# A two-layer hybrid decoder on one core: projection blocks with products of 512 and 256 columns, one more scanning pair, and a new order of the pieces

## The chip, the cores and the metric

The kernel runs on one core of one Trainium2 chip, in one launch. The metric is the device time of the whole program in microseconds; the time before is the median of three runs. In the profile PE is TensorE (matmuls), PEld its weight loads, DVE is VectorE, ACT is ScalarE, POOL is GpSimd and SP is the engine whose queue issues most DMAs.

## What is computed

Two layers on x (256 tokens, 1024 features) with 256 memory tokens. In each layer the normed x is multiplied by one wide weight matrix, whose columns belong to three groups of heads: six stick-breaking heads ("sb"), six MoBA heads ("mb", which at this length is causal softmax attention with rotary embedding), and four heads that attend to the memory tokens ("mem"). Each group is gated by silu of its own gate columns, all are joined and multiplied by w_out, and the result is added to x. A norm closes the program. All of it is float32. Cut to what matters:

```python
for layer in range(DEPTH):                                   # 2
    h = rms_norm(x, norm_g[layer])
    proj = jnp.einsum('btd,dc->btc', h, w_in[layer])         # 1024 x 3584
    sb_q, sb_k, sb_v, sb_g, mb_q, mb_k, mb_v, mb_g, mem_q, mem_g = jnp.split(proj, split_at, axis=-1)
    o_sb = merge_heads(stick_breaking_attention(q, k, v)) * jax.nn.silu(sb_g)
    # per head: z = q k' / 8; log_beta = log_sigmoid(z); log_one_minus = where(past, log_beta - z, 0)
    #   later = reverse cumsum over keys of log_one_minus, less itself
    #   out = where(past, exp(log_beta + later), 0) @ v
    o_mb = merge_heads(moba_attention(partial_rotary(mb_q), partial_rotary(mb_k), mb_v)) * jax.nn.silu(mb_g)
    m = rms_norm(mem, mem_norm_g[layer])
    mk, mv = jnp.split(jnp.einsum('bmd,dc->bmc', m, w_mem_kv[layer]), 2, axis=-1)
    o_mem = merge_heads(memory_attention(mem_q, mk, mv)) * jax.nn.silu(mem_g)
    x = x + jnp.einsum('btc,cd->btd', jnp.concatenate([o_sb, o_mb, o_mem], -1), w_out[layer])
return rms_norm(x, final_norm_g)
```

## The kernel before

**Products in three parts.** A float32 operand is split into two parts of type float32r: hi is the value rounded, lo the rest. A float32 product is made of three: hi*hi, hi*lo and lo*hi, accumulated in one PSUM bank. The activations lie in T tiles of 512 columns per step k of the contraction (eight steps of 128): columns 0 to 255 hold hi for the 256 tokens, 256 to 511 hold lo. Ts lists for each tile its hi half, its lo half and the whole (X[0], X[1], X[2] in the helpers).

**Weights.** w_in, w_mem_kv and w_out come in pieces (one for sb_q, one for sb_g, and so on) in the order that ORDER gives for each layer, then wo0, wo1 and wo2 for the output projection. A piece is cut into chunks of 128 x 768 values (the first four are halves). SP issues their loads, six raw buffers deep; hi_task casts a chunk to hi on ACT or DVE, lo_task makes lo by a subtraction on DVE and then issues the next load. Seven split chunks (tiles hl) can stand ahead of TensorE. At given chunks other loads are put in between: the transposed x (X_AT), the two halves of x (X0_AT, X1_AT) and the constants (CST_AT).

**Blocks.** A piece whose result is wanted transposed (queries and keys of sb and mem, and all gates) is made by T_piece: for each block of 128 of its columns a bank, and in it eight calls of tr_k, each three products of 256 columns. The layer has 18 such blocks, both layers 36. The others (v, and q and k of mb) are made by N_piece, with products of 384 or 256 columns. sb_qk of layer 0 is done first and differently: all six blocks at once, step k by step k, as the weights arrive. Then a block is evacuated: evac_T for queries and keys, gate_evac for gates, by one move on ACT or DVE, and in layer 0 with a multiply by the row norms rbx.

**Attention.** For each pair of heads pair_scores takes two banks and makes the scores, with products on half of the array's rows; pair_task multiplies the weights by V, on half of its columns. SCG and PVG list which pairs are issued together. In layer 0 the sb pairs get the running sum by products with a constant triangle (pair_sums, tiles neg and ah; sb_head does the elementwise part), and give the weights already transposed (wT). In layer 1 the sum is a scan on DVE (scan_head), and the weights are turned as those of the other heads are: 32x32 transposes on DVE into D, a store to DRAM (Z) and four loads back (pair_turn, trip), which SP issues; HALVES names the pairs for which these are eight. The result, times the gate, is split into mxhi and mxlo, the input of the output projection, which takes its eight steps k in the order KORD.

**What sets the order.** All instructions of each engine are issued in an order that a planner finds when the program is built: Sched runs the tasks (generators) against a clock for each engine and a cost for each instruction, with priorities (PRI, P_...), lateness of TensorE tasks (..._LATE), thresholds on free banks (SPARE1, SPARE2, CROWD) and the time at which each buffer is freed. _avail says when a task could go on: from k.t, the end of its last instruction, its inputs and the buffers it asks for. The main task issues all full products in order; before each block it asks for a bank in a step that issues nothing, and its first product is asked for in the next step.

Of the kernel before, what the change touches and what calls it, by code (L numbers as in the profile page):

```python
# [10 lines left out]
AF = mybir.ActivationFunctionType  # L11
OP = mybir.AluOpType
# [15 lines left out]
RAW = 6  # L28
KORD = ((0, 1, 2, 3, 4, 5, 6, 7), (6, 7, 4, 5, 0, 1, 2, 3))
LAT_SAME, LAT_CROSS = 130.0, 240.0  # L30
PE_LATE = 400.0
NORM_LATE = 1234.4
DG_LATE = 544.9
COLD = 3900.0
PRI = {"sb": (44, 10), "mb": (8, -6), "mem": (22, 22)}
P_EV = 37
P_H0 = -8
P_RX = 37
P_M0 = 12
P_RM = 37  # L40
P_M1 = 0
URG = 2
X_AT = {5: 4, 6: 5, 7: 6, 8: 7}
CST_AT = 14
X0_AT = 11
X1_AT = 16
DMA_GBS = 330.0
# [5 lines left out]
TRIP_LAT = 1500.0  # L53
MEM_AT = 0
ORDER = (["sb_qk", "mb_k", "mb_q", "mem_q", "mk", "mv", "sb_v", "mb_g", "sb_g", "mb_v", "mem_g"],
         ["mv", "mk", "mb_q", "mb_k", "mem_q", "sb_q", "sb_k", "mb_v", "mem_g", "mb_g", "sb_g", "sb_v"])
GATES = {"sb_g": ((0,), (1,), (2,)), "mb_g": ((0,), (1,), (2,)), "mem_g": ((0,), (1,))}
SCG = (((("sb", 0), ("sb", 1)), (("mb", 0),), (("mb", 2), ("sb", 2)), (("mb", 1), ("mem", 1)), (("mem", 0),)),
       ((("mb", 1), ("mb", 2), ("mb", 0)), (("mem", 1), ("mem", 0)), (("sb", 0), ("sb", 2)), (("sb", 1),)))
PVG = (((("sb", 0),), (("sb", 1), ("mb", 0), ("mb", 1)), (("sb", 2), ("mb", 2)), (("mem", 0), ("mem", 1))),  # L60
       ((("sb", 2), ("mb", 0)), (("mb", 1), ("mem", 0), ("mem", 1)), (("sb", 0),), (("mb", 2),), (("sb", 1),)))
HOLD = 10396.4
HALVES = [("F", 1, "mb", 1), ("F", 1, "mem", 0), ("F", 0, "mb", 2), ("F", 0, "mem", 1)]
CROWD = 2
SPARE1 = 2
SPARE2 = 1
DVE_W = 554.2
AHEAD = 2
DVE_HI = 671.6
SLACK_PE = 36.4  # L70
SLACK = 89.6

# [24 lines left out]
class Sched:  # L97
# [86 lines left out]
    def run(self):  # L184
        while self.tasks:
            cands = []
            for k in self.tasks:
                prio = k.prio() if callable(k.prio) else k.prio
                best = None
                for eng, cost in k.req["eng"]:  # L190
                    a = self._avail(k, eng)
                    if a is None:
                        continue
                    s = max(a, self.T[eng])
                    if best is None or s + cost < best[0]:
                        best = (s + cost, s, eng)
                if best:
                    cands.append((best[1], prio, best[2], k))
            assert cands, [(k.gen.__name__, k.req) for k in self.tasks]
            s0, _, eng0, _ = min(cands, key=lambda c: (c[0], c[1]))  # L200
            slack = SLACK_PE if eng0 == "pe" else SLACK
            cands = [c for c in cands if c[2] == eng0 and c[0] <= s0 + slack]
            if eng0 == "pe":
                cands = self._by_form(cands)
            _, _, eng, k = min(cands, key=lambda c: (c[1], c[0]))
            if eng == "pe":
                self.form = k.req.get("form", "full")
                self.held.pop(k, None)
            t = self._avail(k, eng)
            bufs = []  # L210
            for tag in k.req.get("alloc", ()):
                b = self.res[tag].best()
                self.res[tag].items.remove(b)
                bufs.append(b[2])
            k.t0 = t
            self._step(k, (eng, bufs))
# [3 lines left out]
def hybrid_trunk(ctx: ExitStack, tc: tile.TileContext, x, mem, norm_g, w_in, w_mem_kv, w_out,  # L220
# [26 lines left out]
    def mm(out, lhsT, rhs, start, stop, **kw):  # L247
        n = _free(rhs)
        half = lhsT.shape[0] == 64 or out.shape[0] == 64
        if lhsT.dtype == FR:  # L250
            c = max(111.0, n * 0.4167 + (20.0 if n > 384 else 13.0))
# [4 lines left out]
        nc.tensor.matmul(out, lhsT=lhsT, rhs=rhs, start=start, stop=stop, **kw)  # L256
# [76 lines left out]
    spare = [sb(f"F{i}", [128, 768]) for i in range(2)]  # L333
    S.res["wT"] = Res([f[:, o:o + 384] for f in spare for o in (0, 384)])
    S.res["Fs"] = Res([])
    S.res["D"] = Res([sb(f"D{i}", [128, 1024]) for i in range(2)])
# [332 lines left out]
    def pair_scores(l, kind, c):  # L669
# [8 lines left out]
        if kind == "mem":  # L678
            regs = [(slice(0, 256), slice(0, 128), slice(0, 256)), (slice(256, 512), slice(128, 256), slice(0, 256))]
        elif kind == "sb" and l == 0:  # L680
# [3 lines left out]
        st, mv_ = (ks[kind], qs[kind]) if kind == "sb" and l == 0 else (qs[kind], ks[kind])  # L684
        for j, (o, a, b) in enumerate(regs):
            for h in range(2):
# [5 lines left out]
                mm(out, st[r, c, a], rhs, j == 0, j == 1)  # L692
        if kind != "sb" or l:
            place[l, kind, c] = len(place)
# [4 lines left out]
    def sb_head(l, h):  # L699
# [14 lines left out]
        stt(a, z, 0.0, a, OP.max, OP.add)  # L714
        e, (hl,) = yield R(("act", 320.0), ("dve", 200.0), alloc=["ah"], cond=lambda: 3 * l + h // 2 <= turn["sb"])
        copy(hl[0], a, e)
# [118 lines left out]
    def pair_task(l, kind, c):  # L835
# [7 lines left out]
        for q, i in group:  # L843
            need += [("wT", l, q, 2 * i), ("wT", l, q, 2 * i + 1)] if q == "sb" and l == 0 else [("F", l, q, i)]
            need.append((VN[q], l))
# [3 lines left out]
        n = 4 if kind == "mem" else 3  # L849
        sums = kind == "sb" and l == 0  # L850
        if sums:
            w2 = [wTs.pop((l, kind, 2 * c + b)) for b in range(2)]
# [3 lines left out]
        for j in range(2):  # L856
            q0 = 0 if j == 0 or kind == "mem" else 128
            for b in range(2):
                out = o[b * 64:b * 64 + 64, q0:256]
                if sums:  # L860
                    rhs = w2[b][:, 256 * j:256 * j + 256 - q0]
# [205 lines left out]
    def main():  # L1067
# [26 lines left out]
        for l in range(DEPTH):  # L1094
# [40 lines left out]
            for kind, n in (("sb", 3), ("mb", 3), ("mem", 2)):  # L1135
                for c in range(n):
                    S.spawn(pair_scores(l, kind, c), PRI[kind][0] + 2)
                    S.spawn(pair_sums(l, c) if kind == "sb" and l == 0 else pair_turn(l, kind, c), PRI[kind][0] + 1)
                    S.spawn(pair_task(l, kind, c), PRI[kind][0])
            if l == 0:  # L1140
# [4 lines left out]
                for k in range(KT):  # L1145
                    if k < 4:
                        groups = [range(3), range(3, 6)] if k < 2 else [range(6)]
                        for g in groups:
                            j, o = p.loc(k, g[0] * 128)
                            o -= g[0] * 128  # L1150
                            steps = [(his, 0, [("hi", j), ("h", 0, "hi", k)]), (his, 1, [("h", 0, k)]),
                                     (los, 0, [("lo", j)])]
                            for w, h, need in steps:
                                prog["cur"] = max(prog["cur"], j)
                                yield R("pe", need=need)
                                for c in g:
                                    mm(accs[c][:, 0:256], w[j % LEAD][:, o + c * 128:o + c * 128 + 128], hT[h][:, k, :],
                                       k == 0 and h == 0 and w is his, False)
# [123 lines left out]
```

## Time and profile before

| | us |
|---|---|
| median of three runs | 274.12 |
| lowest, highest | 274.1, 275.38 |
| profiled execution: device time | 274.33 |
| its span, first to last instruction | 272.6 |
| PE busy | 263.5 |
| DVE busy | 224.0 |
| ACT busy | 194.9 |

The span is what the profile's times are measured in; the device time of the same execution is 1.7 us longer. A group's row reads: line, engine, operation, what it writes from what it reads, shapes, count, then busy time in all, mean ns of one instruction, and the idle time before them with what ended it. A mean of PE holds its pipeline, so the rate of a stream of products is read from the starts in the timeline. A row of the windows has, for each engine, busy us and in brackets the number of instructions, then the granted clock, the busy share of the DMA engines and GB/s.

### The profile page before, as it was taken

How to read it: one execution, taken by the hardware profiler on the slowest of the kernel's cores; microseconds unless marked ns; L12 is line 12 of the kernel's file. 1: busy time of each engine (PE TensorE's matmuls, PEld its weight loads, DVE VectorE, ACT ScalarE, POOL GpSimd, SP SyncE). 2: the span in 40 equal slices, each digit the busy share in tenths (PEclk: the TensorE clock that was granted, in tenths of full speed). 3: DMA queues.
4: the chain of work that ended last, by engine and by line, in shares of the span. 5: the costliest groups of instructions: out<-in, count | busy, mean ns of one | idle time of the engine just before them, and what ended most of it. 6: DMA issues, size and time to landing. Idle time of an engine off the chain costs nothing.

```text
span 272.6 us, 5581 instructions
## 1 busy us (share of the span) xinstructions
PE 263.5 (97%) x1943; PEld 252.8 (93%) x1943; DVE 224.0 (82%) x507; ACT 194.9 (72%) x461; POOL 7.2 (3%) x19
## 2 busy tenths in 40 slices
PE   8999999999979999999999999999999999999991
PEld 5999999999879998998999999999999989988991
DVE  4688986899878999994879587699999999984282
ACT  3578976798897998780875446497989999843053
POOL 0002020200000000000000000000000000000000
PEclk9999999999999999999999999999999999999997
DMA  6999989979954968987294966986798789990004
GB/s 206 353 367 374 390 277 351 301 226 296 265 208 116 268 170 204 340 239 249 74 300 146 303 198 226 273 266 188 248 267 247 257 248 262 315 304 16 2 0 154
DMA packets 49995, 64.74 MB, mean 238 GB/s; under 512 B 4208, under 2 KB 46064, under 8 KB 49968
## 3 DMA queue, kind: packets, MB, share of 16 engines
q1 hardware_dynamic: 48880, 62.29, 73.3%
q0 software_dynamic: 512, 1.31, 1.6%
q10 hardware_dynamic: 576, 0.79, 0.8%
q8 instruction: 15, 0.25, 0.3%
q14 instruction: 12, 0.10, 0.1%
HBM read 56.12 MB, written 8.26 MB: 236 GB/s over the span
## 4 chain that ended last, share of the span: by engine, by line
PE 90%; DMA 4%; DVE 3%; ACT 1%; SPq 0%; issue 0%; DVEq 0%
PE bank L256 90%; DMA raw<-in_w_in_dram 4%; DVE w L781 1%; PE bank L262 1%; DVE st L794 0%; SPq L363 0%; DVE D L828 0%; DVE hl L279 0%; ACT hl L273 0%; ACT ss L275 0%; ACT junk L275 0%; DVE xs L287 0%; DVEq L1278 0%; DVE bank L283 0%; DVE st L803 0%
## 5 line engine op out<-in xcount | busy, mean ns | idle before, releaser
L279 DVE TENSOR_TENSOR hl<-raw,hl 128x768 fp32r<-128x768 f32 (+3 forms) x113 | 101.4, 905 | 12.8 <-ACT hl L273 12.1
L256 PE MATMUL bank<-T,hl 128*128 128x256 f32 x864 | 107.4, 285 | 2.4 <-DVE st L781 2.2
L256 PEld LDWEIGHTS bank<-T,hl 128*128 128x128 f32 x864 | 105.5, 193 | 4.0 <-DVE st L781 2.3
L273 ACT CAST hl<-raw 128x768 fp32r<-128x768 f32 (+3 forms) x101 | 80.1, 802 | 15.1 <-PE bank L256 9.7
L256 PE MATMUL bank<-hl,T 128*128 128x384 f32 (+1 forms) x480 | 81.0, 325 | 0.0
L256 PEld LDWEIGHTS bank<-hl,T 128*128 128x128 f32 x480 | 78.0, 189 | 0.5 <-issue 0.3
L256 PE MATMUL bank<-hl,mxhi 128*128 128x384 f32 (+1 forms) x192 | 45.4, 319 | 0.0
L256 PEld LDWEIGHTS bank<-hl,mxhi 128*128 128x128 f32 x192 | 33.3, 189 | 0.9 <-issue 0.7
L256 PE MATMUL bank<-hl,mxlo 128*128 128x384 f32 (+1 forms) x96 | 30.4, 317 | 0.0
L275 ACT ACTIVATE w<-w,st 128x256 f32<-128x256 f32 (+1 forms) x54 | 22.3, 459 | 1.7 <-DVE st L781 1.1
L275 ACT ACTIVATE junk<-xs 128x384 bf16<-128x384 f32 (+2 forms) x15 | 7.9, 529 | 21.4 <-DVE xs L279 21.0
L275 ACT ACTIVATE ga<-ga 128x256 f32<-128x256 f32 x48 | 19.3, 425 | 0.3 <-DVE ga L283 0.2
L256 PEld LDWEIGHTS bank<-hl,mxlo 128*128 128x128 f32 x96 | 18.1, 189 | 0.0
L828 DVE STREAM_TRANSPOSE D<-w 128x384 f32<-128x384 f32 (+1 forms) x26 | 15.6, 607 | 0.3 <-ACT w L275 0.2
L275 ACT ACTIVATE T<-uT,gc 128x256 fp32r<-128x256 f32 x24 | 11.7, 502 | 4.0 <-DMA uT<-xT_dram 4.0
L275 ACT ACTIVATE a<-a 128x384 f32<-128x384 f32 x24 | 12.0, 529 | 0.0
L279 DVE TENSOR_TENSOR xs<-bank,xs 128x384 f32<-128x384 f32 (+1 forms) x11 | 5.7, 518 | 7.7 <-PE bank L256 7.7
L283 DVE SCALAR_TENSOR_TENSOR T<-uT,gc,T 128x256 fp32r<-128x256 f32 x24 | 11.4, 478 | 0.7 <-ACT T L275 0.6
L275 ACT ACTIVATE w<-bank,st 128x256 f32<-128x256 f32 x16 | 7.4, 476 | 2.5 <-DVE st L794 2.5
L279 DVE TENSOR_TENSOR ev<-bank,gT 128x256 f32<-128x256 f32 x16 | 6.6, 419 | 3.1 <-PE bank L256 3.1
L275 ACT ACTIVATE a<-bank 128x384 f32<-128x384 f32 x18 | 8.4, 492 | 0.5 <-DVE bank L283 0.5
L294 DVE CAST hl<-raw 128x768 fp32r<-128x768 f32 (+1 forms) x12 | 6.0, 498 | 3.0 <-DMA raw<-in_w_in_dram 2.7
(119 smaller groups left out, 231.2 us busy)
## 6 DMA issues: line engine op xcount, KB each, us to landing
raw<-in_w_in_dram SPq DMA_DIRECT2D x70, 384.0 KB, 5.0
raw<-in_w_out_dram SPq DMA_DIRECT2D x19, 384.0 KB, 5.3
Z<-D SPq DMA_DIRECT2D x13, 384.0 KB, 4.9
raw<-in_w_mem_kv_dram SPq DMA_DIRECT2D x8, 384.0 KB, 5.1
uT<-memT_dram SPq DMA_DIRECT2D x8, 256.0 KB, 5.9
Z<-D SPq DMA_DIRECT2D x4, 512.0 KB, 5.6
T<-Z SPq DMA_DIRECT2D x16, 96.0 KB, 5.1
F<-Z SPq DMA_DIRECT2D x12, 96.0 KB, 4.9
```

Source lines behind the costliest of these rows:

```text
L256: nc.tensor.matmul(out, lhsT=lhsT, rhs=rhs, start=start, stop=stop, **kw)
L262: nc.tensor.transpose(out, in_, idt)
L273: nc.scalar.copy(out, in_)
L275: nc.scalar.activation(out, in_, func, **kw)
L279: nc.vector.tensor_tensor(out, a, b, op=op)
L283: nc.vector.scalar_tensor_tensor(out, a, s, b, op0=op0, op1=op1)
L294: nc.vector.tensor_copy(out, in_)
L781: nc.vector.tensor_tensor_reduce(w[:, r0:r1], sc[:, r0:r1], cmask[:, 256 - r1 + r0:256], -1.0, 3.0e38, OP.add, OP.min, st[:, t:t + 1])
L828: nc.vector.transpose(o, w[:, :n * 128].rearrange("p (m j r) -> p m j r", j=4, r=32))
```

## The change

Nine pieces, 26 of the 36 transposed blocks, are listed in DBL: mem_g, mb_g, sb_qk and mk of layer 0; mb_g, mem_q, mk, sb_q and sb_g of layer 1. For these a step k is two products: the hi weights times hi and lo of the activations side by side (512 columns, a whole bank), and the lo weights times hi, added into the second half. The bank then holds hi*hi in one half and the two small products in the other; ACT copies the second half out and DVE adds the first to it. The multiply by the row norms stays, as an instruction of its own.

SUMP = (1, 2) leaves two sb pairs of layer 0 with the sums on TensorE; pair 0 scans as in layer 1. The buffers follow: one of two spare tiles holds wT halves, the other is a turned pair's from the start.

In the planner a task that has been given its buffers now counts from the time at which it got them. The planner charges a product of over 384 columns 3 ns less than before. The orders and groups (ORDER, KORD, GATES, SCG, PVG), the places of the loads and the thresholds have new values.

```diff
-KORD = ((0, 1, 2, 3, 4, 5, 6, 7), (6, 7, 4, 5, 0, 1, 2, 3))
+KORD = ((4, 5, 0, 1, 2, 3, 6, 7), (6, 7, 4, 5, 0, 1, 2, 3))
...
-CST_AT = 14
-X0_AT = 11
-X1_AT = 16
+CST_AT = 12
+X0_AT = 6
+X1_AT = 13
...
-MEM_AT = 0
-ORDER = (["sb_qk", "mb_k", "mb_q", "mem_q", "mk", "mv", "sb_v", "mb_g", "sb_g", "mb_v", "mem_g"],
-         ["mv", "mk", "mb_q", "mb_k", "mem_q", "sb_q", "sb_k", "mb_v", "mem_g", "mb_g", "sb_g", "sb_v"])
-GATES = {"sb_g": ((0,), (1,), (2,)), "mb_g": ((0,), (1,), (2,)), "mem_g": ((0,), (1,))}
-SCG = (((("sb", 0), ("sb", 1)), (("mb", 0),), (("mb", 2), ("sb", 2)), (("mb", 1), ("mem", 1)), (("mem", 0),)),
-       ((("mb", 1), ("mb", 2), ("mb", 0)), (("mem", 1), ("mem", 0)), (("sb", 0), ("sb", 2)), (("sb", 1),)))
-PVG = (((("sb", 0),), (("sb", 1), ("mb", 0), ("mb", 1)), (("sb", 2), ("mb", 2)), (("mem", 0), ("mem", 1))),
-       ((("sb", 2), ("mb", 0)), (("mb", 1), ("mem", 0), ("mem", 1)), (("sb", 0),), (("mb", 2),), (("sb", 1),)))
-HOLD = 10396.4
-HALVES = [("F", 1, "mb", 1), ("F", 1, "mem", 0), ("F", 0, "mb", 2), ("F", 0, "mem", 1)]
-CROWD = 2
+MEM_AT = 1
+ORDER = (["sb_qk", "mb_k", "mb_q", "mem_q", "mv", "sb_g", "mk", "mb_v", "mb_g", "sb_v", "mem_g"],
+         ["mv", "mk", "mb_q", "mb_k", "mem_q", "sb_q", "sb_k", "mb_g", "mb_v", "sb_v", "mem_g", "sb_g"])
+GATES = {"sb_g": ((0,), (1,), (2,)), "mb_g": ((0, 1), (2,)), "mem_g": ((0,), (1,))}
+SCG = (((("mem", 1), ("mb", 0), ("sb", 2)), (("sb", 0), ("sb", 1)), (("mb", 1),), (("mb", 2), ("mem", 0))),
+       ((("sb", 1), ("mb", 2), ("sb", 2)), (("sb", 0), ("mb", 0), ("mb", 1)), (("mem", 0), ("mem", 1))))
+PVG = (((("mem", 0), ("mem", 1)), (("mb", 0), ("mb", 2), ("mb", 1), ("sb", 2)), (("sb", 1), ("sb", 0))),
+       ((("sb", 2),), (("mb", 2), ("sb", 0), ("sb", 1)), (("mb", 0), ("mb", 1), ("mem", 1), ("mem", 0))))
+HOLD = 25950.0
+HALVES = [("F", 0, "mem", 0), ("F", 0, "mb", 1), ("F", 0, "mb", 2)]
+CROWD = 1
...
+SUMP = (1, 2)
+DBL = (("mem_g", 0), ("mb_g", 1), ("mb_g", 0), ("mem_q", 1), ("mk", 1), ("sb_qk", 0), ("sb_q", 1), ("mk", 0), ("sb_g", 1))
...
-            k.t0 = t
+            k.t, k.t0, k.eng = t, t, None
...
-    S.res["wT"] = Res([f[:, o:o + 384] for f in spare for o in (0, 384)])
-    S.res["Fs"] = Res([])
+    nsp = 2 if len(SUMP) == 3 else 1
+    S.res["wT"] = Res([f[:, o:o + 384] for f in spare[:nsp] for o in (0, 384)])
+    S.res["Fs"] = Res(spare[nsp:])
...
         hi, lo = his[j % LEAD], los[j % LEAD]
+        if (p.name, p.layer) in DBL:
+            last = k == KT - 1
+            if last:
+                mm(acc[:, 256:512], lo[:, o:o + 128], X[0][:, k, :], False, False)
+            mm(acc, hi[:, o:o + 128], X[2][:, k, :], k == 0, last)
+            if not last:
+                mm(acc[:, 256:512], lo[:, o:o + 128], X[0][:, k, :], False, False)
+            return
...
-        if l or not soon("rx"):
+        if (kind + "_g", l) in DBL:
+            yield R("act", need=[n for n in need if n != "rx"])
+            act(gT[:, k, :], acc[:, 256:512])
+            yield R("dve")
+            tt(gT[:, k, :], acc[:, 0:256], gT[:, k, :], OP.add)
+            S.free("bank", acc)
+            if not l:
+                yield R("dve", need=["rx"])
+                tt(gT[:, k, :], gT[:, k, :], rbx, OP.mult)
+        elif l or not soon("rx"):
...
-                S.spawn(scan_head(l, h) if l else sb_head(l, h), PRI["sb"][1] + h)
+                S.spawn(sb_head(l, h) if sums(l, "sb", h // 2) else scan_head(l, h), PRI["sb"][1] + h)
...
+                            dbl = ("sb_qk", 0) in DBL
+                            if k and dbl:
+                                steps[:2] = [(his, 2, [("hi", j), ("h", 0, k)])]
```

evac_T is changed for its pieces as gate_evac is, with the scale of the queries in the two instructions. pair_scores, pair_sums, pair_turn and pair_task ask sums(l, kind, c) where they asked for sb in layer 0.

More of the change, by code (lines that the diff above doesn't have):

```diff
@@ L28 @@
 RAW = 6
-KORD = ((0, 1, 2, 3, 4, 5, 6, 7), (6, 7, 4, 5, 0, 1, 2, 3))
+KORD = ((4, 5, 0, 1, 2, 3, 6, 7), (6, 7, 4, 5, 0, 1, 2, 3))
 LAT_SAME, LAT_CROSS = 130.0, 240.0
-PE_LATE = 400.0
-NORM_LATE = 1234.4
-DG_LATE = 544.9
+PE_LATE = 368.2
+NORM_LATE = 542.1
+DG_LATE = 1595.9
 COLD = 3900.0
-PRI = {"sb": (44, 10), "mb": (8, -6), "mem": (22, 22)}
+PRI = {"sb": (12, 16), "mb": (2, 14), "mem": (54, 40)}
 P_EV = 37
 P_H0 = -8
[L38 to L41, printed above, removed]
+P_RX = 27
+P_M0 = 62
+P_RM = 2
+P_M1 = 55
 URG = 2
 X_AT = {5: 4, 6: 5, 7: 6, 8: 7}
-CST_AT = 14
-X0_AT = 11
-X1_AT = 16
+CST_AT = 12
+X0_AT = 6
+X1_AT = 13
 DMA_GBS = 330.0
@@ L53 @@
 TRIP_LAT = 1500.0
-MEM_AT = 0
-ORDER = (["sb_qk", "mb_k", "mb_q", "mem_q", "mk", "mv", "sb_v", "mb_g", "sb_g", "mb_v", "mem_g"],
-         ["mv", "mk", "mb_q", "mb_k", "mem_q", "sb_q", "sb_k", "mb_v", "mem_g", "mb_g", "sb_g", "sb_v"])
-GATES = {"sb_g": ((0,), (1,), (2,)), "mb_g": ((0,), (1,), (2,)), "mem_g": ((0,), (1,))}
-SCG = (((("sb", 0), ("sb", 1)), (("mb", 0),), (("mb", 2), ("sb", 2)), (("mb", 1), ("mem", 1)), (("mem", 0),)),
-       ((("mb", 1), ("mb", 2), ("mb", 0)), (("mem", 1), ("mem", 0)), (("sb", 0), ("sb", 2)), (("sb", 1),)))
-PVG = (((("sb", 0),), (("sb", 1), ("mb", 0), ("mb", 1)), (("sb", 2), ("mb", 2)), (("mem", 0), ("mem", 1))),
-       ((("sb", 2), ("mb", 0)), (("mb", 1), ("mem", 0), ("mem", 1)), (("sb", 0),), (("mb", 2),), (("sb", 1),)))
-HOLD = 10396.4
-HALVES = [("F", 1, "mb", 1), ("F", 1, "mem", 0), ("F", 0, "mb", 2), ("F", 0, "mem", 1)]
-CROWD = 2
+MEM_AT = 1
[9 more added lines that the diff above has]
+CROWD = 1
 SPARE1 = 2
 SPARE2 = 1
[L67 to L71, printed above, removed]
+SUMP = (1, 2)
+DBL = (("mem_g", 0), ("mb_g", 1), ("mb_g", 0), ("mem_q", 1), ("mk", 1), ("sb_qk", 0), ("sb_q", 1), ("mk", 0), ("sb_g", 1))
+DVE_W = 231.1
+AHEAD = 1
+DVE_HI = 718.2
+SLACK_PE = 7.9
+SLACK = 64.5
 def _free(ap):
@@ L250, in mm @@
         if lhsT.dtype == FR:
-            c = max(111.0, n * 0.4167 + (20.0 if n > 384 else 13.0))
+            c = max(111.0, n * 0.4167 + (17.0 if n > 384 else 13.0))
         elif lhsT.dtype == BF:
@@ L651, in hybrid_trunk, with sums @@
     begun = []
+    def sums(l, kind, c):
+        return l == 0 and kind == "sb" and c in SUMP
     done = {"pv": 0}
@@ L679, in pair_scores @@
             regs = [(slice(0, 256), slice(0, 128), slice(0, 256)), (slice(256, 512), slice(128, 256), slice(0, 256))]
-        elif kind == "sb" and l == 0:
+        elif sums(l, kind, c):
             regs = [(slice(0, 256), slice(0, 128), slice(0, 256)), (slice(256, 384), slice(128, 256), slice(128, 256))]
@@ L683, in pair_scores @@
             regs = [(slice(0, 128), slice(0, 128), slice(0, 128)), (slice(128, 384), slice(128, 256), slice(0, 256))]
-        st, mv_ = (ks[kind], qs[kind]) if kind == "sb" and l == 0 else (qs[kind], ks[kind])
+        st, mv_ = (ks[kind], qs[kind]) if sums(l, kind, c) else (qs[kind], ks[kind])
         for j, (o, a, b) in enumerate(regs):
@@ L692, in pair_scores @@
                 mm(out, st[r, c, a], rhs, j == 0, j == 1)
-        if kind != "sb" or l:
+        if not sums(l, kind, c):
             place[l, kind, c] = len(place)
@@ L714, in sb_head @@
         stt(a, z, 0.0, a, OP.max, OP.add)
-        e, (hl,) = yield R(("act", 320.0), ("dve", 200.0), alloc=["ah"], cond=lambda: 3 * l + h // 2 <= turn["sb"])
+        e, (hl,) = yield R(("act", 320.0), ("dve", 200.0), alloc=["ah"], cond=lambda: SUMP.index(h // 2) <= turn["sb"])
         copy(hl[0], a, e)
@@ L843, in pair_task @@
         for q, i in group:
-            need += [("wT", l, q, 2 * i), ("wT", l, q, 2 * i + 1)] if q == "sb" and l == 0 else [("F", l, q, i)]
+            need += [("wT", l, q, 2 * i), ("wT", l, q, 2 * i + 1)] if sums(l, q, i) else [("F", l, q, i)]
             need.append((VN[q], l))
@@ L849, in pair_task @@
         n = 4 if kind == "mem" else 3
-        sums = kind == "sb" and l == 0
-        if sums:
+        summed = sums(l, kind, c)
+        if summed:
             w2 = [wTs.pop((l, kind, 2 * c + b)) for b in range(2)]
@@ L859, in pair_task @@
                 out = o[b * 64:b * 64 + 64, q0:256]
-                if sums:
+                if summed:
                     rhs = w2[b][:, 256 * j:256 * j + 256 - q0]
@@ L868, in pair_task @@
                 mm(out, V[:, j, 2 * c + b, :], rhs, j == 0, j == 1)
-        if sums:
+        if summed:
             for wT in w2:
@@ L872, in pair_task @@
             done["pv"] += 1
-            if done["pv"] == 3:
-                for f in spare:
+            if done["pv"] == len(SUMP):
+                for f in spare[:nsp]:
                     S.free("Fs", f)
@@ L998, in evac_T @@
         dst = (qs if name in ("sb_q", "mem_q") else ks)[kind][:, c, :]
-        if rb is None or not soon(rneed):
+        if ("sb_qk" if l == 0 and kind == "sb" else name, l) in DBL:
+            sc = scale if rb is None else 1.0
+            yield R("act", need=need)
+            if sc == 1.0:
+                act(dst, acc[:, 256:512])
+            else:
+                act(dst, acc[:, 256:512], AF.Copy, scale=sc)
+            yield R("dve")
+            stt(dst, acc[:, 0:256], sc, dst, OP.mult, OP.add)
+            S.free("bank", acc)
+            if rb is not None:
+                yield R("dve", need=[rneed])
+                stt(dst, dst, scale, rb, OP.mult, OP.mult)
+        elif rb is None or not soon(rneed):
             yield R("act", "dve", need=need)
@@ L1137, in main @@
                     S.spawn(pair_scores(l, kind, c), PRI[kind][0] + 2)
-                    S.spawn(pair_sums(l, c) if kind == "sb" and l == 0 else pair_turn(l, kind, c), PRI[kind][0] + 1)
+                    S.spawn(pair_sums(l, c) if sums(l, kind, c) else pair_turn(l, kind, c), PRI[kind][0] + 1)
                     S.spawn(pair_task(l, kind, c), PRI[kind][0])
@@ L1156, in main @@
                                 for c in g:
-                                    mm(accs[c][:, 0:256], w[j % LEAD][:, o + c * 128:o + c * 128 + 128], hT[h][:, k, :],
+                                    half = 256 if dbl and (w is los or h == 1) else 0
+                                    mm(accs[c][:, half:512 if h == 2 else half + 256], w[j % LEAD][:, o + c * 128:o + c * 128 + 128], hT[h][:, k, :],
                                        k == 0 and h == 0 and w is his, False)
```

## The prediction

> **What bounds the kernel now.** I read the page first, then the chain of work that ended last, the waits of TensorE, its timeline, and last the groups by shape and the windows. Busy shares of the page:
>
> ```profile
> span 272.6 us, 5581 instructions
> PE 263.5 (97%) x1943; PEld 252.8 (93%) x1943; DVE 224.0 (82%) x507; ACT 194.9 (72%) x461; POOL 7.2 (3%) x19
> ```
>
> A busy TensorE can still be a waiting one, so the chain decides:
>
> ```profile
> 13.11 0.84 ACT hl L273
> ...
> 13.98 0.97 DVE hl L279
> ...
> 14.99 55.79 PE bank L256 x398
> ...
> 75.65 0.49 DVE D L828
> ...
> 76.58 64.72 PE bank L256 x483
> ...
> 147.72 119.36 PE bank L256 x879
> 267.08 0.02 issue
> ```
>
> Until 14.99 us the loads and the split of weight chunks set the time. From there to 267.08 the chain is TensorE, but for one stretch of DVE before 76.58. After 267.08 come 5.5 us of final norm and store that the change leaves alone. The only long wait of TensorE:
>
> ```profile
> PE bank L256 <- DVE st L781: 2.2, 1, 2.2
> ```
>
> So a product taken off TensorE between 14.99 and 267.08 shortens the kernel, unless something else runs out of slack.
>
> **What a product costs.** The time from the start of one group to that of the next, divided by its count:
>
> ```profile
> 40.13 11.67 PE L256 MATMUL bank<-T,hl 128*128 128x256 f32 x96
> 51.64 1.60 PE L256 MATMUL bank<-hl,T 128*128 128x256 f32 x12
> ...
> 151.15 16.81 PE L256 MATMUL bank<-hl,T 128*128 128x384 f32 x96
> 167.80 7.34 PE L256 MATMUL bank<-T,hl 128*128 128x256 f32 x60
> ```
>
> 256 columns: 11.51/96 = 119.9 ns. 384 columns: 16.65/96 = 173.4 ns. The slope is 53.5/128 = 0.418 ns a column, and 119.9 - 256 x 0.418 = 12.9 ns is fixed for each product.
>
> **The change, part by part.**
>
> *Doubled blocks.* DBL names nine pieces with 2+3+3+2+2+6+3+2+3 = 26 column blocks. Each has eight steps of three 256-column products; now they are one of 512 and one of 256, as many columns with one product less. Nothing in the trace has 512 columns of this type; by the line it takes 173.4 + 128 x 0.418 = 226.9 ns, and a step saves 359.7 - 346.8 = 12.9 ns. Its bounds: nothing, if 512 columns cost two products of 256 (239.8), and 12.9. The row of 384 is the nearest and lies on the line with no step in it, so I take 12.9. (The code's own planner charges 4 ns more above 384 columns; that would make it 8.9.) Of 208 steps the first 24 (four steps k of the six sb_qk blocks) lie ahead of 14.99 us, where loads set the time. 184 x 12.9 = 2.37 us saved.
>
> The Trainium skill ("TensorE: Matmul & The Clock Gate", Back-to-back issue gap) speaks against this term: it gives a warm gap of N/2.4 + 2.5 ns, so that one product less would be worth 2.5 ns, and the term 184 x 2.5 = 0.46 us, an estimate from that page. The row of 256 columns differs: 119.9 ns against 109.2 by that formula; the measurement decides.
>
> *Evacuation of these blocks.* Each bank now holds two halves: ACT copies one, DVE adds the other. Before, one move by either engine did, and for layer 0's gates one DVE multiply from the bank.
>
> ```profile
> L273 ACT COPY gT<-bank 128x256 f32<-128x256 f32 x6 | 2.3, 385 | 0.6 <-PE bank L256 0.6
> L279 DVE TENSOR_TENSOR gT<-bank,rbx 128x256 f32<-128x256 f32 x8 | 3.4, 419 | 2.5 <-PE bank L256 2.4
> L294 DVE COPY gT<-bank 128x256 f32<-128x256 f32 x2 | 0.8, 412 | 0.0
> L287 DVE TENSOR_SCALAR sb_q<-bank 128x256 f32<-128x256 f32 x2 | 0.8, 416 | 0.0
> L294 DVE COPY mem_k<-bank 128x256 f32<-128x256 f32 x1 | 0.4, 425 | 1.7 <-PE bank L256 1.7
> ```
>
> Twenty of the 26 blocks fall where attention runs (53 to 243 us): 20 adds x 0.42 = 8.4 us of DVE, less the five moves of DVE in the last three rows, 2.1: 6.3 us more. A bank is held about 0.8 us instead of 0.4 after its last product.
>
> *Pair 0 of layer 0 scans.* TensorE loses its eight products with neg, one of three such groups:
>
> ```profile
> 61.16 1.25 PE L256 MATMUL bank<-ah,neg 128*128 128x384 f32 x8
> 62.25 4.91 PE L256 MATMUL bank<-hl,T 128*128 128x384 f32 x27
> ```
>
> 62.25 - 61.16 = 1.09 us saved. DVE pays. A scanning head costs the first five rows, a summing head the last three:
>
> ```profile
> L279 DVE TENSOR_TENSOR bank<-bank,smask 128x256 f32<-128x256 f32 x6 | 2.2, 418 | 0.0
> L761 DVE TENSOR_TENSOR_SCAN a<-a,a 128x256 f32<-128x256 f32 x6 | 4.1, 677 | 0.0
> L761 DVE TENSOR_TENSOR_SCAN a<-a,a 128x128 f32<-128x128 f32 x6 | 2.5, 417 | 0.0
> L279 DVE TENSOR_TENSOR w<-bank,a 128x384 f32<-128x384 f32 x6 | 3.3, 548 | 0.1
> L828 DVE STREAM_TRANSPOSE D<-w 128x384 f32<-128x384 f32 x18 | 10.0, 563 | 0.0
> ...
> L283 DVE SCALAR_TENSOR_TENSOR bank<-neg,bank 128x256 f32<-128x256 f32 x6 | 2.3, 422 | 0.0
> L283 DVE SCALAR_TENSOR_TENSOR a<-bank,a 128x384 f32<-128x384 f32 x6 | 3.2, 554 | 0.1
> L279 DVE TENSOR_TENSOR ah<-a,ah 128x384 fp32r<-128x384 f32 x6 | 3.2, 556 | 0.1
> ```
>
> 2.62 - 1.53 = 1.09 us, twice: 2.2 us. The pair also makes a trip through DRAM: one store, four loads and a wait for the store's landing, in SP's queue, with the weight loads behind. HALVES gives eight extra loads less in layer 1, four more in layer 0. A landing is bounded by zero and by
>
> ```profile
> Z<-D SPq DMA_DIRECT2D x13, 384.0 KB, 4.9
> ```
>
> 4.9 us; split weights stand up to seven chunks ahead, each 18 products x 119.9 = 2.2 us of work, so I take zero. That cover goes if DVE's splits fall behind.
>
> *Waits for buffers are planned; pieces and groups are reordered.* The planner used to forget the wait of a task that had taken a bank and issued nothing yet, as the main stream does before each block. On the chip that is the one stall:
>
> ```profile
> 73.60 0.82 PE L256 MATMUL bank<-sb_q,sb_k 64*128 64x256 f32 x8
> 76.58 13.69 PE L256 MATMUL bank<-T,hl 128*128 128x256 f32 x112 [2.15 <-DVE st L781]
> ```
>
> Six score pairs were issued in a row, twelve banks of eight, and the next block had none until DVE had read some. In the new order scores come in groups of 3, 2, 1 and 2 pairs, and the main stream's wait counts. It saves between nothing and 2.15 us, or costs as much again if it comes twice. I take 2.15, because after the start the waits show no second one of its size, wherever the plan did count. What is late next is the gates of sb_g, now layer 1's last piece: from a block's last product to its mxlo stand eleven instructions of about 0.41 us as in the rows above, 4.5 us, and k = 0 and 1 of the output products are due 16 x 0.347 + 12 x 0.1734 = 7.6 and 8 x 0.347 + 15 x 0.1734 = 5.4 us after their block. I cost it at zero; hand-overs could add 1.5 us. In layer 0 the four summing heads have two wT buffers instead of four for six: pair 2 can't leave its banks before pair 1's values are multiplied, after sb_v. What hides it are mem_g's 16 steps, 5.5 us; zero again, with the same 1.5 us if they don't suffice. MEM_AT moves nothing, as no block is issued between its two places.
>
> Runs of half-array products are broken into from full products:
>
> ```profile
> 177.00 8.89 PE L256 MATMUL bank<-T,hl 128*128 128x256 f32 x72
> 185.82 2.24 PE L256 MATMUL bank<-uT 64*128 64x128 f32 x24
> ```
>
> 8.82 - 72 x 0.1199 = 0.19 us for the two switches. Eleven runs now; 13 groups after against 18, merged or not, so 9 to 13 runs: -0.4 to +0.4, taken as zero.
>
> *Loads moved.* x's first half moves from behind chunk 11 to behind chunk 6, the second from 16 to 13, the constants from 14 to 12, all in SP's queue ahead of weights. In the start the queue is full:
>
> ```profile
> 0.00:15.00 15.00, 13.56 (x89) 11.41 (x89) 8.51 (x17) 7.47 (x12) 0.66 (x8) 1.00 0.85 291
> 15.00:53.00 38.00, 38.00 (x274) 38.00 (x274) 31.15 (x69) 30.23 (x67) 5.46 (x9) 1.00 1.00 342
> 53.00:243.00 190.00, 187.85 (x1426) 180.40 (x1424) 169.90 (x387) 148.52 (x361) 1.12 (x2) 1.00 0.80 240
> ```
>
> 0.524 MB at 342 GB/s is 1.53 us in front of chunk 7. Its split ends at 16.30 now,
>
> ```profile
> 15.34 0.96 DVE L279 TENSOR_TENSOR hl<-raw,hl 128x768 fp32r<-128x768 f32 x1
> ```
>
> then at 17.83, and its products are due at 14.99 + 6 x 0.347 = 17.07: 0.76 us lost (between 0 and 1.5). Later chunks gain 0.4 us of slack each.
>
> **Sum.** -2.37 - 1.09 - 2.15 + 0.76 = -4.85 us. The profiled execution took 274.33 (span 272.6 and 1.7 around it), so 269.5; the median of the runs, 274.12, is 0.2 lower: 269.3.
>
> **Rivals.**
>
> *The bank wait stays*, or another like it comes: groups of three pairs take six of eight banks at once, and DVE has more to do before it frees one. 269.3 + 2.15 = 271.5. For it: the new first group is such a one. Against: the wait is now counted.
>
> *The doubled product saves nothing*, because 512 columns cost 239.8 ns: 269.3 + 2.37 = 271.7. The rows of 256 and 384 speak against it. By the page's 2.5 ns it would be 269.3 + 1.91 = 271.2, an estimate.
>
> *Slower: DVE becomes the bound between 53 and 243 us.* It has 169.9 us of work there and 20.1 idle. It gets 6.3 + 2.2 = 8.5 more, 178.4, while TensorE's stretch shrinks to about 190 - 2.15 - 1.09 - 2.06 (20 x 8 x 12.9 ns) = 184.7: 6.3 us left. If as much idle as now cannot be used, the stretch is 198.5 and the time 269.3 + 13.8 = 283.1. It is slower than before by over 0.5% once 12.5 of the 20.1 stay idle, and no faster than by 0.5% from 9.7. Against it:
>
> ```profile
> 199.00:220.00 21.00, 21.00 (x158) 20.89 (x157) 20.27 (x41) 19.77 (x49) 0.00 (x0) 1.00 0.87 251
> ```
>
> DVE can run with 0.7 us idle in 21 and TensorE doesn't stall; and ACT, 148.5 of 190 busy, can take casts from it.
>
> **How the numbers follow.** 0.5% (1.4 us) is about what a measurement of this kernel can tell from no change; its runs lie between 274.1 and 275.38. Forecast as summed (267 to 271): 0.53. Bank wait: 0.18. No saving by doubling: 0.07. DVE bound in part (272.75 to 275.5): 0.12, in full: 0.10. So faster 0.78, same 0.12, slower 0.10. Low end: all 208 steps gain (-0.31), no start loss (-0.76), fewer switches (-0.4), some of the hand-over before 14.99: 267.2. High end: bank wait and no doubling gain together, 273.8; beyond it lies most of the DVE case.
>
> **What would show it.** Steps of 512+256 at 347 ns; two groups with neg; no idle of TensorE near 2 us between 53 and 113; 0.8 us idle near 17. Wrong if TensorE waits for hl (splits late), for mxhi or mxlo at the start of an output projection, or for a bank; or if DVE's idle in attention stays near 20 us.

## The result and the profile after

The changed kernel takes 270.93 us (270.57 to 271.72) against 274.11 on the same chip: 0.988 of the kernel before, 95% interval 0.9841 to 0.9919. On a second chip, where it ran again beside the experiments, it is 0.9855 (0.9834 to 0.9876): 270.1 us. By the medians it is 3.2 and 4.5 us faster; 269.3 us was forecast. The 58 executions of the kernel before beside the experiments form two groups, 27 of 273.4 to 274.1 us with a mean granted clock of 0.994 to 0.996 and 31 of 274.5 to 275.6 us with 0.988 to 0.991; none of the changed program's fifteen lies under 0.994.

The page of its profiled execution (271.06 us):

```profile
span 269.0 us, 5193 instructions
PE 261.0 (97%) x1733; PEld 241.0 (90%) x1733; DVE 229.4 (85%) x532; ACT 197.9 (74%) x462; POOL 7.3 (3%) x19
```

There are 210 products fewer: 202 of doubled steps (26 blocks of eight, less the first step of each of sb_qk's six blocks, which keeps its three products) and eight with neg. DVE has 5.4 us more. The chain of work that ended last:

```profile
1.19 94.31 PE bank L258 x612
95.50 0.02 issue
95.53 0.14 ACT sb_v L277
...
96.01 0.63 ACT ga L277
...
96.66 0.34 DVE gT L281
...
97.27 0.42 DVE ga L285
97.69 0.34 DVE st L809
98.03 0.30 SPq L366
...
99.38 0.45 SPq L1007
...
99.87 5.91 DMA T<-Z
...
105.92 32.53 PE bank L258 x227
...
146.25 117.46 PE bank L258 x777
263.71 0.02 issue
```

TensorE carries it from 1.19, without the loads that stood at its head before. It leaves TensorE once, from 95.5 to 105.92: an evacuation on ACT, gates and a reduction on DVE, SP's queue, and the landing of a pair's turned tile. TensorE's longest wait, and the timeline at that place:

```profile
PE bank L258 <- DMA T<-Z: 1.5, 1, 1.5
```

```profile
102.42 2.03 PE L258 MATMUL bank<-T,hl 128*128 128x512 f32 x10
105.92 2.17 PE L258 MATMUL bank<-T,mb_v 128*64 128x256 f32 x24 [1.47 <-DMA T<-Z]
```

The stall of 2.15 us for a bank near 74 us is gone; no wait follows the scores:

```profile
68.16 1.58 PE L258 MATMUL bank<-uT 64*128 64x128 f32 x16
69.58 1.03 PE L258 MATMUL bank<-mem_k,mem_q 64*128 64x256 f32 x8
70.53 8.61 PE L258 MATMUL bank<-hl,T 128*128 128x384 f32 x48
```

The price of a doubled step, from 46 products (23 steps, ended by one switch to half-array products, 0.09 us):

```profile
165.58 8.22 PE L258 MATMUL bank<-T,hl 128*128 128x512 f32 x46
173.73 2.00 PE L258 MATMUL bank<-mem_k,mem_q 64*128 64x256 f32 x16
```

(173.73 - 165.58 - 0.09)/23 = 350.4 ns against 3 x 119.9 = 359.7: 9.3 ns saved a step. The first block of that stretch takes 347.1 ns a step and the second 352.1 (starts at 165.58, 168.36 and 171.17); why is open.

Last, the first block of mb_k, which stands behind sb_qk and so tells the start; before, then after:

```profile
23.48 6.75 PE L256 MATMUL bank<-hl,T 128*128 128x384 f32 x38
```

```profile
22.82 16.83 PE L258 MATMUL bank<-hl,T 128*128 128x384 f32 x96
```

TensorE's last product ends 3.37 us earlier (267.08 to 263.71). Of this 202 x 9.3 ns = 1.9 are doubled steps, 1.09 the eight products with neg, 0.68 the smaller wait (2.15 to 1.47), and 0.27 the start (23.48 - 22.82 = 0.66, of which the 42 doubled steps of sb_qk are 0.39). That makes 3.94, 0.6 too much. The half-array products now come in twelve runs and not eleven, worth 0.19 by the prediction's price of a run; the rest is not accounted for. The start is the least certain of these terms, since mb_k starts at 22.37 to 22.82 us in three executions of the changed program.

### The profile page after: what moved, and what is told of

It reads as the page before. It is cut to its first block, busy times and chain, and to the rows that moved or that the text cites. A ratio compares the mean times of both kernels' runs of the same rounds, so it can differ in the third digit from the quotient of the medians.

```text
span 269.0 us, 5193 instructions
## 1 busy us (share of the span) xinstructions
PE 261.0 (97%) x1733; PEld 241.0 (90%) x1733; DVE 229.4 (85%) x532; ACT 197.9 (74%) x462; POOL 7.3 (3%) x19
## 4 chain that ended last, share of the span: by engine, by line
PE 94%; DMA 2%; ACT 1%; DVE 1%; SPq 1%; issue 0%; DVEq 0%
PE bank L258 93%; DMA T<-Z 2%; PE bank L264 1%; SPq L1007 1%; ACT ga L277 0%; ACT ss L277 0%; ACT junk L277 0%; DVE ga L285 0%; DVE xs L289 0%; DVE gT L281 0%; DVE st L809 0%; DVEq L1319 0%; SPq L366 0%; DVE junk L1107 0%; ACT sb_v L277 0%
## 5 line engine op out<-in xcount | busy, mean ns | idle before, releaser
L258 PE MATMUL bank<-T,hl 128*128 128x256 f32 (+1 forms) x662 | 106.7, 320 | 0.0
L258 PEld LDWEIGHTS bank<-T,hl 128*128 128x128 f32 x662 | 94.1, 192 | 10.2 <-issue 1.8
L275 ACT CAST hl<-raw 128x768 fp32r<-128x768 f32 (+2 forms) x108 | 83.9, 795 | 11.2 <-PE bank L258 8.2
L277 ACT ACTIVATE w<-w,st 128x256 f32<-128x256 f32 (+1 forms) x44 | 18.9, 464 | 2.4 <-DVE st L796 2.2
L277 ACT ACTIVATE ga<-ga 128x256 f32<-128x256 f32 (+1 forms) x42 | 18.5, 446 | 1.1 <-DVE ga L285 0.7
L843 DVE STREAM_TRANSPOSE D<-w 128x384 f32<-128x384 f32 (+1 forms) x28 | 17.0, 606 | 0.9 <-ACT w L277 0.9
L277 ACT ACTIVATE a<-bank 128x384 f32<-128x384 f32 x20 | 9.4, 485 | 0.1
L776 DVE TENSOR_TENSOR_SCAN a<-a,a 128x256 f32<-128x256 f32 (+1 forms) x16 | 8.5, 536 | 0.0
L796 DVE CUSTOM_DVE_ANT_0 w<-bank,cmask 128x128 f32<-128x128 f32 (+1 forms) x24 | 7.5, 348 | 0.2 <-PE bank L258 0.2
```

What stands on the lines that cost most here:

```text
L275: nc.scalar.copy(out, in_)
L277: nc.scalar.activation(out, in_, func, **kw)
L776: nc.vector.tensor_tensor_scan(a[:, r0:r1], a[:, r0:r1], u[:, r0:r1], 0.0, OP.add, OP.add)
L796: nc.vector.tensor_tensor_reduce(w[:, r0:r1], sc[:, r0:r1], cmask[:, 256 - r1 + r0:256], -1.0, 3.0e38, OP.add, OP.min, st[:, t:t + 1])
L843: nc.vector.transpose(o, w[:, :n * 128].rearrange("p (m j r) -> p m j r", j=4, r=32))
```

## Experiments

The kernel before ran beside every group of kernels (274.7, 274.59 and 274.1 us), and ratios are to it. The changed kernel for comparison is 0.9855 to 0.988.

**The doubling by itself.** First with nothing else moved: the changed kernel's order on every engine, and three products where there are two.

```diff
-            mm(acc, hi[:, o:o + 128], X[2][:, k, :], k == 0, last)
+            # the planner's cost is that of one product of 512
+            mm(acc[:, 0:256],   hi[:, o:o + 128], X[0][:, k, :], k == 0, False)
+            mm(acc[:, 256:512], hi[:, o:o + 128], X[1][:, k, :], False, last)
```

> The changed kernel with its order on every engine, but each of the 202 doubled steps issued as three products of 256 columns into the same two halves of the bank; evacuation, scans, groups and loads stay. Theory A (TensorE sets the time, and the doubling's worth is the product it saves): in the changed kernel's trace a step takes 350 ns against 360, so 202 x 9.7 = 2.0 us more TensorE work. About 88 of these steps lie ahead of the wait for a turned tile at 104 us, which does not hang on TensorE and would swallow their 0.85 us: 270.9 + 1.1 = 272.0 (271.7 to 272.9), and the wait at 104 shrinks from 1.5 to about 0.7 us. Theory B (the gain came from order and waits, TensorE has room): 270.9, and other waits of TensorE shrink too.

273.35 us, 0.9973 (0.9944 to 1.0003): about 1% over the changed kernel, 2.4 to 3.2 us by the medians. It missed high, and the wait grew where it was to shrink. Behind the wait the clock fell to half for 3.4 us (in a row of windows the granted clock is the third value from the end):

```profile
PE bank L263 <- DMA T<-Z: 2.3, 1, 2.3
```

```profile
107.20:110.60 3.40, 3.40 (x25) 2.66 (x22) 2.26 (x7) 0.00 (x0) 0.00 (x0) 0.50 1.05 404
```

In the profiled executions the last product ends 3.04 us later than in the changed kernel (266.75 against 263.71). The wait is 0.8 us of this. From the products behind it (106.39, against 105.92) to the products with mv (the rows below) k1 takes 1.7 us longer, nearly all of it the half clock. From those rows to the last product neither kernel waits, and both have the full clock; the changed kernel's row stands first:

```profile
120.73 1.95 PE L258 MATMUL bank<-T,mv 128*64 128x256 f32 x16
```

```profile
122.90 1.95 PE L263 MATMUL bank<-T,mv 128*64 128x256 f32 x16
```

263.71 - 120.73 = 142.98 us against 266.75 - 122.90 = 143.85: 0.87 us for the 104 doubled steps of layer 1, 8.4 ns a step. So theory A's mechanism holds where nothing else differs; the difference of the whole times also has the longer wait and the half clock in it and is not the doubling's price. Why the tile came later is open: its loads were issued at 98.49 us (98.38 in the changed kernel) and took 6.3 us to land (5.9).

Then without doubling, planned anew:

```diff
-DBL = (("mem_g", 0), ("mb_g", 1), ...)
+DBL = ()
```

> The changed kernel with DBL empty: no block doubled, one move for each evacuation, and the plan made anew with the changed kernel's parameters. Theory A: TensorE's 2.0 us come back, less what an easier DVE (26 adds of 0.42 us fewer) takes off waits: 272 to 273.5. Theory B (the adds on DVE cost what the products save): 270.9 or less.

275.63 us, 1.0045 (1.0019 to 1.0072): slower than the kernel before, and above the 272 to 273.5 of theory A. Besides the products it has waits for mxhi and mxlo of 0.3 and 0.5 us at the start of the output projections, so the changed kernel's parameters, planned anew without doubled blocks, bring no gain.

And the kernel before with doubling alone:

```diff
 # the kernel before, with its parameters and its planner
+SUMP = (0, 1, 2)
+DBL = (("mem_g", 0), ("mb_g", 1), ...)   # the same nine pieces
```

> The kernel before, with the doubling alone: its parameters, three summing pairs, waits for buffers not planned, and the changed kernel's nine pieces doubled. Theory A: 274.1 - 2.0 = 272.1, with the stall of 2.2 us near 74 still there, 273 if the added DVE work lengthens it. Theory B: 274.1 or more, since DVE, full in attention, gets 26 adds.

271.74 us, 0.9905 (0.9883 to 0.9926): 2.6 us off, most of what the whole change brings, though not by the doubled products alone. The stall near 74 went with it, though the planner here doesn't count the wait: its plan now puts five score pairs and not six in a row, and the next block starts without a wait.

```profile
68.18 2.16 PE L258 MATMUL bank<-mem_k,mem_q 64*128 64x256 f32 x16
70.26 2.38 PE L258 MATMUL bank<-hl,T 128*128 128x384 f32 x12
```

**The counted wait.** The changed kernel itself, the changed kernel with the planner's old line, and the kernel before with the new one.

> The changed kernel itself, for comparison on the same chip as the three others of this group: 0.988 of the kernel before, and a wait of 1 to 2 us of TensorE near 104 us for a turned tile.

270.1 us, 0.9855; the wait near 104 us is 1.0 us in this execution.

```diff
-            k.t, k.t0, k.eng = t, t, None
+            k.t0 = t
```

> The changed kernel with the planner's old line, in which a task that got its buffers does not count the time at which it got them; all else planned anew. Theory A (the counted wait is what took away the stall near 74 us): a wait of TensorE for DVE of 1 to 2.5 us in a block behind a run of scores, and 272 to 273.5. Theory B (that stall was a matter of which groups follow one another, and counting the wait does nothing by itself): the changed kernel's time within 0.8 us, no wait for a bank over 0.5 us.

The plan comes out the same, instruction for instruction on all engines. The 271.01 us, 0.9872 (0.9848 to 0.9895), are a further measurement of the same program, and show how far two lie apart.

```diff
 # the kernel before
-            k.t0 = t
+            k.t, k.t0, k.eng = t, t, None
```

> The kernel before with the planner's new line alone. Theory A: the stall near 74 us goes or shrinks, 272 to 273.5. Theory B: the same groups follow one another, so the stall of about 2 us stays, 274 to 275.

275.19 us, 1.0025 (1.0007 to 1.0042), and the stall is where it was, with the clock at half behind it:

```profile
72.55 0.82 PE L256 MATMUL bank<-sb_q,sb_k 64*128 64x256 f32 x8
75.53 4.75 PE L256 MATMUL bank<-T,hl 128*128 128x256 f32 x25 [2.15 <-DVE st L781]
```

```profile
75.60:79.10 3.50, 3.50 (x17) 3.50 (x18) 3.13 (x13) 3.50 (x14) 0.00 (x0) 0.51 0.37 146
```

In the kernel before's own profiled execution the same stall of 2.15 us left the clock at 1.00. One such stretch lowers the mean clock of an execution by 3.4 x 0.5/273 = 0.006, about the distance of the two groups of the kernel before, whose times differ by 1.1 us on the mean. So the stall seems to cost more than its length in some executions; the changed program, with waits of 1.0 to 1.5 us in its traces, shows no such stretch. Against the 27 executions without it the changed program's fifteen gain 3.1 us on the mean (273.8 to 270.7), near the 3.37 of the traces. That all 31 executions have their half clock at this place is argued from k6's trace, not shown.

Theory B holds in both: the stall is a matter of which groups follow one another, and counting the wait does nothing to it. In the kernel before the new line changed the plan a little, but not there.

**The scanning pair.**

```diff
-SUMP = (1, 2)
+SUMP = (0, 1, 2)
```

> The changed kernel with all three sb pairs of layer 0 summed on TensorE (and both spare tiles as wT halves); planned anew. Theory A (each summing pair costs TensorE its 1.09 us and DVE had room for the scan): 1.1 us slower than the changed kernel, less if its trip's absence shortens the wait at 104 us. Theory B (the scan's 2.2 us of DVE and its trip in SP's queue cost as much as they save): the same time or up to 1.5 us faster, with the wait at 104 us gone.

271.22 us, 0.9907 (0.9874 to 0.994): by the ratios 1.0 to 1.4 us over the two runs of the changed program on the same chip, by the medians 0.2 to 1.1. Two of its seven executions, of 273.31 and 273.5 us, lift the ratio. The sign fits theory A's 1.09; the intervals overlap, so the size isn't shown by the times.

**The new wait near 104 us.** The plan stays; the loads of three turned pairs are issued whole.

```diff
             for i0 in range(0, 4, 2 if name in HALVES else 4):
-                nc.sync.dma_start(Fv[32 * j:32 * j + 32, i0:i1], ...[j, :, i0:i1])
+                if i0 == 0:
+                    nc.sync.dma_start(Fv[32 * j:32 * j + 32], ...[j])
                 S.op("sp", SP_ISSUE)
```

> The changed kernel with its plan, but the loads of the three turned pairs that HALVES names are issued as four whole ones and not eight halves: twelve issues of about 0.5 us fewer in SP's queue, and nothing else moved. Theory A (the wait of 1.5 us at 104 us comes from SP's queue: the last pair's loads stand behind sixteen half loads between 85 and 96 us): the last loads are issued some 4 us earlier, that wait is gone, 270.9 - 1.5 = 269.4. Rival (the transfers, not their issue, set the landing, or something else is late as well): 270.6 to 271.2 and a wait in the same place.

269.43 us, 0.9823 (0.9799 to 0.9846), as theory A has it. SP's queue in the changed kernel, then here; the last pair's loads are the third and the second of these rows:

```profile
92.52 3.78 SPq L1007 DMA_DIRECT2D T<-Z  x8
96.40 1.93 SPq L366 DMA_DIRECT2D raw<-in_w_out_dram  x4
98.38 1.92 SPq L1007 DMA_DIRECT2D T<-Z  x4
```

```profile
93.25 2.07 SPq L366 DMA_DIRECT2D raw<-in_w_out_dram  x4
95.37 1.88 SPq L1008 DMA_DIRECT2D T<-Z  x4
```

They are issued 3 us earlier, and TensorE goes on without a wait:

```profile
102.33 2.03 PE L258 MATMUL bank<-T,hl 128*128 128x512 f32 x10
104.29 2.17 PE L258 MATMUL bank<-T,mb_v 128*64 128x256 f32 x24
```

This version beats both kernels. Those with more DVE work, with all blocks doubled and with the two products turned round build on it.

**Is DVE full?** A further DVE instruction behind each of the 26 adds, in the plan of the kernel with whole loads.

```diff
             tt(gT[:, k, :], acc[:, 0:256], gT[:, k, :], OP.add)
+            nc.vector.tensor_tensor(gT[:, k, :], gT[:, k, :], gT[:, k, :], op=OP.max)
 # and the same behind the adds of evac_T
```

> The kernel with whole loads and its plan, with one more DVE instruction in place (a maximum of the 256 columns with themselves, 0.42 us) behind each of the 26 adds: 10.9 us more of DVE, 8.4 of it where attention runs. Theory A (TensorE sets the time and DVE's idle time can be used): within 1 us of the kernel with whole loads, 0.982 to 0.986 of the kernel before. Theory B (DVE is full in attention and the plan rests on it): 4 to 11 us slower, with TensorE waiting for hl, mxhi or mxlo.

270.36 us, 0.9866 (0.9844 to 0.9888): by the ratios 1.2 us more than with whole loads, for 26 x 0.426 = 11.1 us of DVE. That is just over theory A's 1 us and far from B. Its windows, in the columns of the prediction's:

```profile
53.00:110.00 57.00, 57.00 (x392) 51.46 (x391) 56.75 (x151) 51.32 (x129) 0.57 (x1) 1.00 0.87 266
...
150.00:243.00 93.00, 92.48 (x615) 83.93 (x614) 86.50 (x210) 70.66 (x165) 0.00 (x0) 1.00 0.79 242
```

From 53 to 110 us DVE is busy for 56.75 of 57 us and TensorE never waits; in layer 1 it waits 0.5 us for hl.

Then all 36 blocks doubled, planned anew:

```diff
-DBL = (("mem_g", 0), ("mb_g", 1), ...)
+DBL = tuple((n, l) for l in range(2) for n in ("sb_qk", "sb_q", "sb_k", "mem_q", "mk", "sb_g", "mb_g", "mem_g"))
```

> The kernel with whole loads, and all 36 transposed blocks doubled; planned anew with the same parameters. Theory A (TensorE sets the time, DVE has room): 80 steps more at 9.7 ns, 0.98 of the kernel before, 268.7. Theory B (with ten adds more DVE is the bound in attention): TensorE waits for split weights or for mxhi and mxlo, and the kernel is 2 to 10 us slower than with 26 blocks.

287.67 us, 1.0498 (1.0473 to 1.0523): slower by far, but not as theory B has it.

```profile
PE bank L258 <- DMA T<-Z: 10.3, 1, 10.3
PE bank L258 <- DVE mxlo L281: 1.2, 1, 1.2
...
PE bank L258 <- DVE mxhi L296: 0.6, 1, 0.6
```

The largest wait is again for a turned tile, which the plan with these parameters brings late. Neither theory forecast such a time. The chain to that tile runs over DVE from 102.65 to 106.64 us, and DVE is busy for 16.40 of the 17 us from 100 to 117 (first row below), so this kernel does not separate the order from the load of DVE. What ten doubled blocks more would bring with a fitting order stays open.

The windows also show the clock:

```profile
100.00:117.00 17.00, 6.70 (x47) 5.16 (x47) 16.40 (x35) 12.18 (x29) 0.00 (x0) 0.82 0.92 262
117.00:127.00 10.00, 9.96 (x60) 8.30 (x61) 3.93 (x12) 0.59 (x1) 0.00 (x0) 0.79 0.24 64
127.00:150.00 23.00, 23.00 (x162) 21.93 (x161) 14.39 (x28) 11.81 (x30) 0.00 (x0) 1.00 0.47 139
```

In the wait and the 10 us behind it the clock is 0.82 and 0.79 on the mean, then 1.00. The Trainium skill ("TensorE: Matmul & The Clock Gate", Part 1: The HAM clock gate) has TensorE at half clock after an idle window of about 3.4 us until some 3.4 us of work have passed. The wait of 10.3 us agrees with it; but waits of 2.15 and 2.3 us were enough in the executions of k6 and k1, and the same 2.15 us were not in the profiled one of the kernel before, so the measurement decides: a wait well under 3.4 us can be followed by half the clock for 3.4 us.

**The loads moved.**

```diff
-CST_AT = 12
-X0_AT = 6
-X1_AT = 13
+CST_AT = 14
+X0_AT = 11
+X1_AT = 16
```

> The changed kernel with x's halves and the constants loaded where they were before (behind chunks 11, 16 and 14); planned anew. Theory A (x's first half in front of chunk 7 costs the start 0.76 us): sb_qk's steps k = 4 and 5 start that much earlier and the first block of mb_k about 0.7 us earlier than the 22.8 us of the changed kernel. Theory B (the loads share the DMA engines and the early half delays nothing that is due): mb_k starts within 0.3 us of 22.8; the time differs from the changed kernel's only by what the new plan does, 270 to 274.

272.73 us, 0.9955 (0.9929 to 0.9981). mb_k starts at 22.12, which by its words fits theory A's 0.7 us before 22.8. But in eight executions of kernels with x early and sb_qk doubled it starts at 22.20 to 22.82, so 22.8 is the last of them. Part of this spread is the rate of the very first products: those of 256 columns start 213 ns apart until 6.9 us in the changed kernel and until 5.4 us here, and about 120 apart from then on. Where they reach the 120 as early as here, by 5.4 us (k9, k10, k11, k12), mb_k starts at 22.37, 22.40, 22.30 and 22.20. So the early half costs the start 0.1 to 0.3 us, no more than executions differ by, and not 0.76. The new plan lost the time elsewhere: two waits for turned tiles, 1.8 us together, are what the trace shows.

**The two products of a step, the other way round,** in the kernel with whole loads.

```diff
-            if last:
+            if k:
                 mm(acc[:, 256:512], lo[:, o:o + 128], X[0][:, k, :], False, False)
             mm(acc, hi[:, o:o + 128], X[2][:, k, :], k == 0, last)
-            if not last:
+            if not k:
                 mm(acc[:, 256:512], lo[:, o:o + 128], X[0][:, k, :], False, False)
```

> The kernel with whole loads and its plan; in each doubled step but the first the product of 256 columns goes ahead of that of 512. Theory A (each product has its own fixed cost): a step stays at 347 to 361 ns, and the time within 0.5 us of the kernel with whole loads. Theory B (the 17 to 20 ns that 512 columns cost beyond their streaming depend on which product is next): steps move by 5 ns or more, the time by 1 us or more.

269.14 us, 0.9817 (0.9792 to 0.9841), the fastest here by a difference that can't be told from none. Busy time and mean of the 512 products, with whole loads and then so:

```profile
L258 PE MATMUL bank<-T,hl 128*128 128x512 f32 x202 | 70.3, 399 | 0.0
```

```profile
L258 PE MATMUL bank<-T,hl 128*128 128x512 f32 x202 | 69.4, 395 | 0.0
```

Doubled steps that follow one another take 351.3 ns on the mean with whole loads and 349.4 so, a difference under theory B's 5 ns. As far as this order can tell, theory A: the cost is the product's own.

## Why the prediction was right and where it was wrong

The direction, the range and the bound held. TensorE set the time, products taken off it came back as time, and DVE took what it was given. The size was too large: 4.85 us summed against 3.2 measured on the first chip, 4.0 by the ratio on the second, and 3.37 at TensorE's last product in the traces. That it came this near is in part luck, as a loss of 0.76 us that did not come hid half of the bank wait's error. By its steps:

- *Doubled blocks.* Mechanism right, size off both ways. A step saves 9.3 ns, or 8.4 between k1 and the changed kernel, and not 12.9: on the mean 512 columns don't lie on the line through 256 and 384, though one block of the stretch shown does. The planner's lower price, 8.9, which I set aside, was nearer. At 9.3 ns all 202 steps are worth 1.9 us, for 2.37. Whether sb_qk's 42 of them count is open: where the first products reach 120 ns at about the same time, mb_k starts at 22.82 with them and 23.08 without (k2), but in another such pair at 22.20 (k12) and 22.18 (k1). Whole times with and without doubling differ by 2.4 to 3.2 us (k1) and 2.6 (k5), since waits and the clock shift with it.
- *The fixed 2.5 ns a product.* The Trainium skill's figure ("TensorE: Matmul & The Clock Gate", Back-to-back issue gap), 0.46 us on its own, does not hold for these products: 9.3 ns a step in the trace, and 8.4 between two kernels of one order.
- *The scanning pair*: 1.09 us forecast. The eight products are gone from the trace; by whole times the pair is worth 0.2 to 1.4 us (k4), so the size is not shown.
- *The bank wait.* This step failed. I had it gone because the planner now counts it. That line changes nothing: the kernel before keeps its stall with it, and the changed kernel's plan is the same without. The order took the stall away, and brought another of 1.5 us. The term was mis-sized too: 2.15 us forecast, 0.68 between the two traces. And it had no price for the half clock that can follow such a stall, as the one trace before the change shows none.
- *The trip through DRAM* was costed at zero, with the weight loads named as what stands behind it. What stood behind SP's queue was another trip: half loads, two for each whole one, delayed the issue of the last pair's loads by 3 us, and TensorE was at its products before the tile. The rival of a wait in place of the one removed was right in size, 1.5 us for 2.15, and wrong in place and cause. With whole loads the time is 269.4, the forecast's number, though not by its terms.
- *Loads moved.* Failed: 0.76 us of loss was forecast, and 0.1 to 0.3 at most is seen. It took the queue as one line with a fixed rate. Nor was the chain of loads before 14.99, on which the count of lost steps rested, a fixed bound: the kernel before with the planner's new line has the same loads there and started mb_k at 22.43, against 23.48. Part of that is again the first products, 120 ns apart from 5.5 us there and from 6.7 us in the kernel before.
- *The gates of sb_g and the two wT buffers*, costed at zero: TensorE waits at neither place.
- *DVE as the bound.* Rejected for this kernel: 11.1 us more of DVE cost 1.2. Its idle time in attention was usable, to 99% in one stretch of 57 us. Its own load was forecast too high: 8.5 us more in attention alone, where the page has 5.4 more in the whole program. The planner gave casts to ACT, as the prediction said it could: DVE's casts to hi went from 12 to 6, ACT's from 101 to 108.

## What to carry to other kernels

Before a planner's better knowledge is credited with the end of a stall, ask which order of work makes that stall: a plan that can do nothing else still waits. A stall's length is not its whole price where the clock can fall behind it, so look at the granted clock of several executions and not of the profiled one alone. In a queue that issues in order, each DMA issue costs what stands behind it, so splitting loads finer can delay the one that is needed. A share of 94% busy on a second engine (k12's DVE, from 53 to 243 us) is no bound by itself; add work to it and see.

## What was not expected of the hardware

A float32r product of 512 columns takes 350.4 - 119.9 = 230.5 ns, its partner counted as before, where the line through 256 and 384 columns gives 226.9. In the start, 0.5 MB put ahead of due loads cost 0.1 to 0.3 us at most. A wait of TensorE of 2.15 us was followed by 3.4 us of half clock in one execution (k6) and by none in another (the kernel before).
